# Token sums behind the next item's splits in a macaron transformer kernel, and a conditioning step that starts later

## The chip, the cores and the metric

The kernel runs on one core of one Trainium2 chip. The metric is the device time of one execution in microseconds; the time before is the median of 3 runs.

## The reference, cut to what matters

Two layers work on 768 tokens of width 1024 (256 context tokens, 512 latent tokens). Each layer is a macaron sandwich: half-step SwiGLU FFN, token mixer, half-step SwiGLU FFN. Shift, scale and gate of each sub-layer come from a conditioning vector (adaLN).

```
mx = silu(c) @ ada_w[i] + ada_b[i]                        # 9 rows of 1024 for each layer
def _ffn_sublayer(h, mod, g_pre, g_post, w_in, w_out):
    u = rmsnorm(h, g_pre) * (1 + scale) + shift
    a, b = split(u @ w_in, 2)                             # first gemm: 1024 -> 2 x 2816
    y = (silu(a) * b) @ w_out                             # second gemm: 2816 -> 1024
    return h + 0.5 * gate * rmsnorm(y, g_post)
```

Everything is float32. There are four FFNs: f00 and f01 before and after the attention of layer 0, f10 and f11 those of layer 1. In f11 only the latent tokens are left.

## The kernel before, in words

**Numbers in two parts.** TensorE multiplies in a float32r format; the kernel writes each operand as hi + lo, where hi is a rounded copy made by ScalarE and lo the difference, made by VectorE (`split`, lines 117 to 127; both instructions carry the lines 123 and 126). Each product is three passes, hi·hi, hi·lo and lo·hi (`mm3`). The weights are loaded by `wraw` (three buffers) and split into `whi` and `wlo` (three buffers each, `wpool`, line 78). A buffer comes free when TensorE has read it.

**The first gemm** (`FirstGemm`, line 425) walks over items. The tokens are two sets of three tiles of 128 (two of two tiles in f11). The later items ("R" and "F", `group`, line 553) use a Strassen-like scheme, which multiplies sums of weight blocks with sums of token blocks, so that one item serves both sets of tokens. The token sums T of the second set are made in `to_sums` (line 308) from the normed tokens; they are not ready when the first gemm starts. So it starts with a head: 7, 7, 6 and 5 "E" items (`EARLY`, line 31, for f00, f01, f10 and f11), which need the first set of tokens alone. During the head VectorE and ScalarE make the T sums of the second set's tiles.

An E item is four products. `early_a` (518) multiplies the two weight halves x = 0, 1 with token features 0 to 511, and ScalarE copies the two results out (L529). `early_b` (536) multiplies the halves with features 512 to 1023; VectorE adds the copies (L544), ScalarE takes Silu of the first (L546), VectorE multiplies the two (L548). All four results come out of the two PSUM buffers `psg` (line 80), so a product waits until one of the results before it has been read. Tile names: f01e5x and f01e5v are the PSUM results of item 5 of f01 in early_a and early_b, f015s0h, f015s0l, f015s1h and f015s1l its split weights (half 0 and 1, hi and lo), f01e5s the sums of L544 and L548.

**The steps by which the token sums go on** are a generator in the list `late`; `late_step` (410) runs it to its next yield. Each E item calls it four times: after each product in early_a, after the Silu in early_b, at the end of early_b. For each tile of the second set `to_sums` has three stages: L322 to L328, L331 to L337, L339 to L341; VectorE does L323, L324, L325, then L331, L332, L334, L335, L337, then L339 and L341. With four calls an item, the last tile's second stage falls on the call after Silu of item 4 in f00, f01 and f10, and its third stage on the end of item 4.

**The splits of the next item** are the generator `prep` (459), run by `step`. early_b of item i calls `self.step(i + 1)` first, which splits half 0 of the next item, and `self.step(i + 1, 9)` near its end, which splits half 1.

**The order on an engine** is not the order of the program text. The framework's scheduler builds each engine's queue ahead of time: of the instructions that its own timing holds to be ready it takes the one traced first. An engine then works through its queue strictly in order. `tc.keep_in_program_order(i)` ties instruction i behind whatever was traced before it on the same engine; it adds no wait beyond the queue's order.

**Conditioning.** `mods_pairs` (215) computes the rows of ada_w for later sub-layers during the groups of f00 (3 pairs of rows), f01 (2) and f10 (3). `group` calls `work.step(1)` twice, in its middle (588) and at its end (608). The generator loads two slices of ada_w (`aw`, 1 MB each, two buffers), one on each of its first two steps; then every second step does 8 + 8 matmuls (L245), an add on VectorE (L249), and loads the next two slices. After each pair there is one more step. At the end of an item with x = 1 the stores of the hidden rows (L606, L607) stand on the sync engine's queue (SP) before the step.

Of the kernel before, what the change touches and what calls it, by code (L numbers as in the profile page):

```python
# [9 lines left out]
F32 = mybir.dt.float32  # L10
# [27 lines left out]
PAT1 = "kqVkkqVV"  # L38
PROG0 = "SF1F2b"
PROG1 = "SF12Fb"  # L40
SUMV = (2, 2, 2, 2)
TURN = 1
EVAC = "AA"
JUNK = 1
# [10 lines left out]
def kernel(  # L55
# [19 lines left out]
    nc = tc.nc  # L75
# [32 lines left out]
    def psum_g(name):  # L108
        return psg.tile([P, 512], F32, tag="g", name=name)
# [94 lines left out]
    def pair_loads(pool, pair, k):  # L204
        w = pool.tile([P, 2, D], F32, tag="aw", name=f"aw{pair[0][0]}{pair[0][1]}{k}")
        rows = slice(k * P, (k + 1) * P)
        if pair[0][0] == pair[1][0]:
            l, m = pair[0]
            nc.sync.dma_start(w, ada_w[l, rows, m * D : (m + 2) * D].rearrange("p (a n) -> p a n", a=2))
        else:  # L210
            for a, (l, m) in enumerate(pair):
                nc.sync.dma_start(w[:, a], ada_w[l, rows, m * D : (m + 1) * D])
        return w

    def mods_pairs(pool, pairs):
        seq = [(pair, k) for pair in pairs for k in range(KC)]
        ws, rows = {}, {}

        def load(q):
            if q >= len(seq):  # L220
                return
            pair, k = seq[q]
            nm = f"{pair[0][0]}{pair[0][1]}"
            if k == 0:
                for x, tag in (("b", "mb"), ("g", "araw")):
                    rows[x] = pool.tile([P, 512], F32, tag=tag, name=f"m{x}{nm}")
                    for a, (l, m) in enumerate(pair):
                        row = ada_b[l, m * D : (m + 1) * D] if x == "b" else norm_g[l, g_index[m]]
                        src = bass.AP(tensor=row.tensor, offset=row.offset, ap=[[512, 2], [0, 32], [1, 512]])
                        nc.sync.dma_start(rows[x][64 * a : 64 * a + 64, :], src)  # L230
            ws[q] = pair_loads(pool, pair, k)

        load(0)
        yield
        load(1)
        yield
        for q, (pair, k) in enumerate(seq):
            if k == 0:
                acc, gg = rows["b"], rows["g"]
            if k % 2 == 0:  # L240
                ps = psum_g(f"am{pair[0][0]}{pair[0][1]}{k}")
                for z in range(2):
                    w = ws.pop(q + z)
                    for c in range(4):
                        nc.tensor.matmul(  # L245
                            ps[32 * c : 32 * c + 32], lhsT=s32[:, k + z],
                            rhs=w[:, c // 2, c % 2 * 512 : c % 2 * 512 + 512], start=z == 0, stop=z == 1,
                        )
                nc.vector.tensor_tensor(out=acc, in0=ps, in1=acc, op=ALU.add)  # L249
                load(q + 2)  # L250
                load(q + 3)
            yield
            if k < KC - 1:
                continue
            for a, (l, m) in enumerate(pair):
                r = slice(64 * a, 64 * a + 64)
                if m % 3 == 1:
                    nc.vector.scalar_tensor_tensor(acc[r], acc[r], 1.0, gg[r], ALU.add, ALU.mult)
                elif m % 3 == 2:
                    nc.vector.scalar_tensor_tensor(acc[r], acc[r], 1.0 if m == 5 else 0.5, gg[r], ALU.mult, ALU.mult)  # L260
                for h in range(2):
                    at = 64 * a + 32 * h
                    nc.sync.dma_start(mdram[l][m][:, h * 512 : h * 512 + 512], acc[at : at + 2, :])
                finished.add((l, m))
            yield
# [23 lines left out]
    def by_turn(tp, cols):  # L289
        for k in range(KC):  # L290
            nc.scalar.activation(tp[:, k], tp[:, k], AF.Identity, scale=cols[:, 1, k : k + 1], bias=cols[:, 0, k : k + 1])
# [16 lines left out]
    def to_sums(pool, t, first, un, ps, sums, name, cols=None):  # L308
        tt, sub, add = nc.vector.tensor_tensor, ALU.subtract, ALU.add
        mine = slice(t * P, (t + 1) * P)  # L310
        twin = slice(first * P, (first + 1) * P)
        hi, lo = uhi.bitcast(F32), ulo.bitcast(F32)
        tp = ps.rearrange("p (k n) -> p k n", k=KC) if un is not None else ps
        if un is not None:
            for k in range(KC):
                nc.tensor.transpose(tp[:, k, :], un[:, k * P : (k + 1) * P], ident)
            by_turn(tp, cols)
            yield
        b12, b22 = tp[:, 0:4, :], tp[:, 4:8, :]
        ta = pool.tile([P, 2, 4, P], F32, tag="R1", name=name + "ta")  # L320
        tb = pool.tile([P, 2, 4, P], F32, tag="R1", name=name + "tb")
        nc.scalar.copy(uhi[:, 4:8, mine], b22)  # L322
        tt(out=ta[:, 0], in0=b12, in1=hi[:, 0:4, twin], op=sub)  # L323
        tt(out=ta[:, 0], in0=ta[:, 0], in1=lo[:, 0:4, twin], op=sub)  # L324
        tt(out=ta[:, 1], in0=b22, in1=ta[:, 0], op=sub)  # L325
        th, tl = sums["T"]
        col = slice((t - sums["t2"]) * P, (t - sums["t2"] + 1) * P)
        nc.scalar.copy(th[:, 0:2, :, col], ta)  # L328
        yield
        t4 = tt if sums["vector"] else nc.gpsimd.tensor_tensor  # L330
        t4(out=tb[:, 1], in0=hi[:, 4:8, twin], in1=ta[:, 1], op=sub)  # L331
        t4(out=tb[:, 1], in0=tb[:, 1], in1=lo[:, 4:8, twin], op=add)  # L332
        nc.scalar.copy(tb[:, 0], b12)
        tt(out=tb[:, 0], in0=b22, in1=tb[:, 0], op=sub)  # L334
        tt(out=tl[:, 0:2, :, col], in0=ta, in1=th[:, 0:2, :, col].bitcast(F32), op=sub)  # L335
        nc.scalar.copy(th[:, 2, :, col], tb[:, 0])
        tt(out=ulo[:, 4:8, mine], in0=b22, in1=hi[:, 4:8, mine], op=sub)  # L337
        yield
        tt(out=tl[:, 2, :, col], in0=tb[:, 0], in1=th[:, 2, :, col].bitcast(F32), op=sub)  # L339
        nc.scalar.copy(uhi[:, 0:4, mine], tb[:, 1])  # L340
        tt(out=ulo[:, 0:4, mine], in0=tb[:, 1], in1=hi[:, 0:4, mine], op=sub)  # L341
        yield
# [67 lines left out]
    def late_step(n=1):  # L410
        for _ in range(n):
            while late:
                if next(late[0], "end") == "end":
                    late.pop(0)
                else:
                    break

    def sums_for(pool, sets, name, f):
        n = len(sets[1]) * P
        return {  # L420
            "t1": sets[0][0], "t2": sets[1][0], "vector": SUMV[f] > 1,
            "T": [pool.tile([P, 3, 4, n], F32R, tag=f"T{x}", name=f"{name}T{x}") for x in "hl"],
        }

    class FirstGemm:
# [110 lines left out]
        def early_b(self, i, g):  # L536
            n, pool, nm = self.n, self.pool, f"{self.nm}e{g}"
            a, p1 = self.ops[i], self.p1[i]
            self.step(i + 1)
            sa = [pool.tile([P, 384], F32, tag="h" + "hl"[x], name=f"{nm}s{x}")[:, 0:n] for x in range(2)]  # L540
            for x in range(2):
                ps = psum_g(f"{nm}v{x}")[:, 0:n]
                self.prod(ps, [y[:, 4:8] for y in a[x]], self.cols(self.t1, 4))
                nc.vector.tensor_tensor(out=sa[x], in0=ps, in1=p1[x], op=ALU.add)  # L544
                if x == 0:
                    nc.scalar.activation(sa[0], sa[0], AF.Silu)  # L546
                    late_step()
            nc.vector.tensor_tensor(out=sa[0], in0=sa[0], in1=sa[1], op=ALU.mult)  # L548
            nc.sync.dma_start(hdr[self.slot][2 * g][:, self.t1 * P : self.t1 * P + n], sa[0])
            self.step(i + 1, 9)  # L550
            late_step()
# [782 lines left out]
    def mods(pool, *pairs):  # L1334
        work.add(mods_pairs(pool, [((m // 10, m % 10), (n // 10, n % 10)) for m, n in pairs]))
# [77 lines left out]
    with Main("m0") as mp:  # L1413
# [40 lines left out]
        def second():  # L1454
            hs = [load_h(mp, t, hin_of(t), f"in{t}") for t in full[1]]
            yield
            for t, h in zip(full[1], hs):
                tp = turned(mp, t, h, f"in{t}")
                yield
                us = mp.tile([P, KC, P], F32, tag="AB"[t % 2] + "0", name=f"us{t}")  # L1460
                by_cols("D", us, tp, 0, KC, 0)
                yield
                yield from to_sums(mp, t, t - 3, None, us, more[1], f"in_{t}")
# [87 lines left out]
```

## Time and profile before

| | us |
|---|---|
| median of 3 runs (2819.9 to 2825.96) | 2823.1 |
| the profiled execution's own time | 2828.1 |
| its span, first to last instruction | 2826.1 |
| TensorE matmuls busy in it | 2737.5 (97%) |
| VectorE busy | 1930.6 (68%) |
| ScalarE busy | 1247.4 (44%) |
| GpSimd busy | 754.4 (27%) |

The span is what the trace covers; all moments below are microseconds from its start. PE is TensorE's matmuls, PEld its weight loads, DVE VectorE, ACT ScalarE, POOL GpSimd, SPq the queue of the sync engine, which issues the DMAs. A matmul is shown longer than the time to the next, since they overlap.

### The profile page before, as it was taken

The page shows a single profiled execution, that of the slowest core. Times are in us where ns is not written, and L with a number is a line of the kernel's source. Part 1 is how long each engine was busy: PE and PEld are TensorE (multiplying, and loading weights), DVE is VectorE, ACT ScalarE, POOL GpSimd, SP SyncE. Part 2 cuts the span into 40 slices and gives each one's busy share as a digit, 9 for nine tenths or more (in the row PEclk, how much of TensorE's full clock was granted, in tenths as well). Part 3 has the DMA queues.
Part 4 walks back from the last instruction along what each step waited for, and adds up shares of the span by engine and source line. Part 5 has one row for each costly group of instructions (what it writes and reads, how often), then busy time and mean ns, then how long its engine had stood idle before and what let it go on. Part 6 is the DMA issues. An engine that isn't in the chain of part 4 may idle for free. (4 is left out here: it accounts for less than half of the span.)

```text
span 2826.1 us, 41442 instructions
## 1 busy us (share of the span) xinstructions
PE 2737.5 (97%) x15928; PEld 2436.6 (86%) x15928; DVE 1930.6 (68%) x2550; ACT 1247.4 (44%) x1999; POOL 754.4 (27%) x639
## 2 busy tenths in 40 slices
PE   7999999999998998999999999999999999989999
PEld 6888998888887788899888978998888887789987
DVE  5777755568778587777554867674655556699965
ACT  5322334345556573233344722333444445644444
POOL 0455411000000014554110354430110110177700
PEclk9999999999999999999999999999999999999999
DMA  8786256543333477832665677326644445654375
GB/s 282 254 300 240 100 189 202 189 140 83 92 107 117 154 233 249 292 127 91 221 212 160 211 273 279 136 97 232 219 148 122 120 120 153 216 169 148 123 247 195
DMA packets 318037, 511.60 MB, mean 181 GB/s; under 512 B 28112, under 2 KB 242000, under 8 KB 310672
## 3 DMA queue, kind: packets, MB, share of 16 engines
q1 hardware_dynamic: 317552, 508.31, 54.7%
q8 instruction: 125, 2.05, 0.3%
q14 instruction: 72, 0.59, 0.1%
q10 hardware_dynamic: 288, 0.66, 0.1%
HBM read 410.19 MB, written 63.05 MB: 167 GB/s over the span
## 5 line engine op out<-in xcount | busy, mean ns | idle before, releaser
L1258 POOL TENSOR_TENSOR bias<-bp,nneg 128x128 f32<-128x128 f32 x112 | 50.0, 485 | 285.7 <-DMA nneg<-in_na_neg 94.3
L126 DVE TENSOR_TENSOR f00hl<-f00h,f00hh 128x384 fp32r<-128x384 f32 x44 | 25.6, 582 | 74.2 <-ACT f00hh L123 74.2
L126 DVE TENSOR_TENSOR f01hl<-f01h,f01hh 128x384 fp32r<-128x384 f32 x44 | 25.3, 575 | 74.6 <-ACT f01hh L123 74.6
L126 DVE TENSOR_TENSOR f10hl<-f10h,f10hh 128x384 fp32r<-128x384 f32 x44 | 26.8, 610 | 68.2 <-ACT f10hh L123 68.1
L123 ACT CAST f01hh<-f01h 128x384 fp32r<-128x384 f32 x44 | 22.6, 515 | 112.6 <-PE f01y L732 94.6
L123 ACT CAST f00hh<-f00h 128x384 fp32r<-128x384 f32 x44 | 22.6, 515 | 111.8 <-PE f00y L732 93.0
L245 PE MATMUL am<-aw,s 128*32 128x512 f32 x512 | 64.4, 611 | 7.5 <-DMA aw<-in_ada_w 7.5
L123 ACT CAST f10hh<-f10h 128x384 fp32r<-128x384 f32 x44 | 22.6, 515 | 100.9 <-PE f10y L732 92.5
L131 PE MATMUL av<-pt,davh 128*128 128x256 f32 x224 | 44.0, 290 | 0.6 <-ACT pt L1180 0.6
L245 PEld LDWEIGHTS am<-aw,s 128*32 128x32 f32 x512 | 12.7, 109 | 35.5 <-issue 22.1
L1320 PE MATMUL nav<-npt,navh 128*64 128x256 f32 (+1 forms) x320 | 39.3, 365 | 0.0
L131 PEld LDWEIGHTS av<-pt,davh 128*128 128x128 f32 x224 | 35.8, 191 | 2.4 <-ACT pt L1180 1.0
L123 ACT CAST f11hh<-f11h 128x256 fp32r<-128x256 f32 x44 | 17.8, 405 | 38.4 <-DMA f11h<-hr 25.7
L126 DVE TENSOR_TENSOR f11hl<-f11h,f11hh 128x256 fp32r<-128x256 f32 x44 | 20.3, 464 | 18.0 <-ACT f11hh L123 17.8
L1320 PEld LDWEIGHTS nav<-npt,navh 128*64 128x64 f32 x320 | 22.0, 136 | 12.2 <-issue 1.9
L1105 POOL TENSOR_TENSOR daq0r<-daq0r,rope 128x512 f32<-128x512 f32 x1 | 1.8, 1798 | 114.6 <-DVE daq0s L1104 114.6
L131 PE MATMUL av<-pt,davl 128*128 128x256 f32 x112 | 31.5, 282 | 0.0
L249 DVE TENSOR_TENSOR mb<-am,mb 128x512 f32<-128x512 f32 x32 | 21.8, 682 | 6.4 <-PE am L245 6.2
L285 POOL TENSOR_SCALAR f00y0r<-f00y0s 128x1 f32<-128x1 f32 x1 | 0.2, 192 | 84.5 <-ACT f00y0j L279 84.5
L285 POOL TENSOR_SCALAR f10y0r<-f10y0s 128x1 f32<-128x1 f32 x1 | 0.2, 192 | 84.5 <-ACT f10y0j L279 84.5
L285 POOL TENSOR_SCALAR f01y0r<-f01y0s 128x1 f32<-128x1 f32 x1 | 0.2, 192 | 84.5 <-ACT f01y0j L279 84.5
L285 POOL TENSOR_SCALAR f01y3r<-f01y3s 128x1 f32<-128x1 f32 x1 | 0.2, 192 | 79.3 <-ACT f01y3j L279 79.3
(9729 smaller groups left out, 11477.8 us busy)
## 6 DMA issues: line engine op xcount, KB each, us to landing
aw<-in_ada_w SPq DMA_DIRECT2D x63, 1024.0 KB
f00r<-in_ffn_w_in SPq DMA_DIRECT2D x22, 1024.0 KB
f01r<-in_ffn_w_in SPq DMA_DIRECT2D x22, 1024.0 KB
f10r<-in_ffn_w_in SPq DMA_DIRECT2D x22, 1024.0 KB
f11r<-in_ffn_w_in SPq DMA_DIRECT2D x22, 1024.0 KB
f00o<-in_ffn_w_out SPq DMA_DIRECT2D x21, 1024.0 KB
f01o<-in_ffn_w_out SPq DMA_DIRECT2D x21, 1024.0 KB
f10o<-in_ffn_w_out SPq DMA_DIRECT2D x21, 1024.0 KB
```

The costliest lines, as they stand in the source:

```text
L123: i = nc.scalar.copy(hi, src)
L126: eng.tensor_tensor(out=lo, in0=src, in1=hi.bitcast(F32), op=ALU.subtract)
L131: nc.tensor.matmul(ps, lhsT=lhs[i], rhs=rhs[j], start=first and n == 0, stop=last and n == 2)
L245: nc.tensor.matmul(ps[32 * c : 32 * c + 32], lhsT=s32[:, k + z], rhs=w[:, c // 2, c % 2 * 512 : c % 2 * 512 + 512], start=z == 0, stop=z == 1,
L249: nc.vector.tensor_tensor(out=acc, in0=ps, in1=acc, op=ALU.add)
L285: nc.gpsimd.tensor_scalar(r, ss, 1.0, EPS, ALU.mult, ALU.add)
L1105: nc.gpsimd.tensor_tensor(out=raw, in0=raw, in1=cs[:, 0, :], op=ALU.mult)
L1258: nc.gpsimd.tensor_tensor(out=bias[:, m, :].rearrange("p (a b) -> p a b", a=8), in0=view, in1=neg[:, m, :].rearrange("p (a b) -> p a b", a ...
L1320: nc.tensor.matmul(av[64 * i : 64 * i + 64, half * 256 + c0 : half * 256 + c0 + n], lhsT=made[u]["v"][0][:, key, vc : vc + 64], rhs=made[u ...
```

## The change

It touches five places. (1) In `to_sums` the first VectorE instruction of each of the three stages (L323, L331, L339) is tied behind what was traced before it on VectorE. (2) In `early_b`, where the next item is an E item, the split of its half 1 is traced after the Silu and before the `late_step` there; where the next item is not, it stays at the end. (3) The generator of `mods_pairs` has one more empty step after its second load. (4) The first two instructions of the second stage always go to VectorE. (5) The constant SUMV, whose four entries were all 2 and so chose VectorE for those two everywhere, goes away.

```diff
-SUMV = (2, 2, 2, 2)
...
     def mods_pairs(pool, pairs):
...
         load(1)
         yield
+        yield
         for q, (pair, k) in enumerate(seq):
...
     def to_sums(pool, t, first, un, ps, sums, name, cols=None):
...
-        tt(out=ta[:, 0], in0=b12, in1=hi[:, 0:4, twin], op=sub)
+        tc.keep_in_program_order(tt(out=ta[:, 0], in0=b12, in1=hi[:, 0:4, twin], op=sub))
...
-        t4 = tt if sums["vector"] else nc.gpsimd.tensor_tensor
-        t4(out=tb[:, 1], in0=hi[:, 4:8, twin], in1=ta[:, 1], op=sub)
-        t4(out=tb[:, 1], in0=tb[:, 1], in1=lo[:, 4:8, twin], op=add)
+        tc.keep_in_program_order(tt(out=tb[:, 1], in0=hi[:, 4:8, twin], in1=ta[:, 1], op=sub))
+        tt(out=tb[:, 1], in0=tb[:, 1], in1=lo[:, 4:8, twin], op=add)
...
-        tt(out=tl[:, 2, :, col], in0=tb[:, 0], in1=th[:, 2, :, col].bitcast(F32), op=sub)
+        tc.keep_in_program_order(tt(out=tl[:, 2, :, col], in0=tb[:, 0], in1=th[:, 2, :, col].bitcast(F32), op=sub))
...
     def early_b(self, i, g):
...
                 if x == 0:
                     nc.scalar.activation(sa[0], sa[0], AF.Silu)
+                    if self.items[i + 1][0] == "E":
+                        self.step(i + 1, 9)
                     late_step()
```

## Rows read from the trace of the kernel before

**Rows 1.** The page, part 1: busy time of PE and DVE.

```profile
PE 2737.5 (97%) x15928; PEld 2436.6 (86%) x15928; DVE 1930.6 (68%) x2550; ACT 1247.4 (44%) x1999; POOL 754.4 (27%) x639
```

**Rows 2.** Busy time by stretch: the heads of f00 (from item 2), f01, f10, f11.

```profile
core 0: us, PE busy (x) PEld busy (x) DVE busy (x) ACT busy (x) POOL busy (x), PEclk, DMA share, GB/s
56.20:103.10 46.90, 44.14 (x256) 42.80 (x256) 43.45 (x59) 26.84 (x42) 12.98 (x6) 1.00 0.66 204
1015.60:1089.00 73.40, 65.01 (x362) 63.10 (x361) 56.45 (x70) 50.65 (x89) 14.66 (x17) 0.95 0.68 211
1552.60:1609.10 56.50, 54.37 (x314) 52.40 (x313) 47.73 (x59) 46.33 (x80) 15.96 (x14) 1.00 0.64 202
2446.20:2493.10 46.90, 37.97 (x261) 35.83 (x262) 37.77 (x48) 33.21 (x61) 12.96 (x12) 0.89 0.56 178
```

**Rows 3.** Waits of PE: for whom, us in total, times, longest.

```profile
PE am L245 <- DMA aw<-in_ada_w: 7.5, 6, 2.9
...
PE f01e5x L131 <- DVE f015s1l L126: 5.7, 1, 5.7
...
PE f00a1W L131 <- DVE mb L249: 1.2, 1, 1.2
...
PE f00e5x L131 <- DVE f005s1l L126: 1.1, 1, 1.1
```

**Rows 4.** Timeline of PE in f01: start, us, ...; items 4 to 6.

```profile
1061.94 0.34 PE L131 MATMUL f01e4v<-o0uh,f014s1l 128*128 128x384 f32 x1
1063.33 0.44 PE L131 MATMUL f01e5x<-o0uh,f015s0h 128*128 128x384 f32 x1 [1.05 <-DVE f01e4s L544]
...
1074.34 0.69 PE L131 MATMUL f01e5x<-o0uh,f015s1l 128*128 128x384 f32 x1 [5.71 <-DVE f015s1l L126]
...
1080.65 0.33 PE L131 MATMUL f01e6x<-o0uh,f016s0h 128*128 128x384 f32 x1
1080.82 0.33 PE L131 MATMUL f01e6x<-o0ul,f016s0h 128*128 128x384 f32 x1
```

**Rows 5.** Timeline of ACT in f01: the rounded copy of that half.

```profile
1060.06 1.05 ACT L123 CAST f015s1h<-f01r 128x1024 fp32r<-128x1024 f32 x1 [1.02 <-PE f01e4v L131]
```

**Rows 6.** Timeline of DVE in f01, items 4 and 5.

```profile
1063.80 0.54 DVE L544 TENSOR_TENSOR f01e4s<-f01e4v,f01e4p 128x384 f32<-128x384 f32 x1
1064.26 0.68 DVE L331 TENSOR_TENSOR o_5tb<-o0uh,o_5ta 128x512 f32<-128x512 f32 x1
...
1070.34 1.74 DVE L341 TENSOR_TENSOR o0ul<-o_5tb,o0uh 128x512 fp32r<-128x512 f32 x1
1072.00 2.28 DVE L126 TENSOR_TENSOR f015s1l<-f01r,f015s1h 128x1024 fp32r<-128x1024 f32 x1
...
1075.34 0.54 DVE L544 TENSOR_TENSOR f01e5s<-f01e5v,f01e5p 128x384 f32<-128x384 f32 x1
```

**Rows 7.** Timeline of DVE in f00, items 4 and 5.

```profile
86.25 0.68 DVE L331 TENSOR_TENSOR in_5tb<-inuh,in_5ta 128x512 f32<-128x512 f32 x1
...
89.05 1.22 DVE L126 TENSOR_TENSOR f005s1l<-f00r,f005s1h 128x1024 fp32r<-128x1024 f32 x1
...
92.53 0.55 DVE L544 TENSOR_TENSOR f00e5s<-f00e5v,f00e5p 128x384 f32<-128x384 f32 x1
```

**Rows 8.** First products of f00's items 5 and 6: starts of first and last matmul.

```profile
L131 PE MATMUL f00e5x<-inuh,f005s0h x4: 334/334/334, 83.8 to 85.3; 128*128 128x384 f32 x4
...
L131 PE MATMUL f00e6x<-inuh,f006s0h x4: 334/334/334, 95.1 to 96.7; 128*128 128x384 f32 x4
```

**Rows 9.** Timeline of PE: conditioning matmuls, the first without a wait, in f00, f01 and f10.

```profile
132.63 1.92 PE L245 MATMUL am<-aw,s 128*32 128x512 f32 x16
...
215.57 1.06 PE L245 MATMUL am<-aw,s 128*32 128x512 f32 x8 [1.15 <-DMA aw<-in_ada_w]
...
1200.61 1.07 PE L245 MATMUL am<-aw,s 128*32 128x512 f32 x8 [1.00 <-DMA aw<-in_ada_w]
...
1642.37 1.59 PE L245 MATMUL am<-aw,s 128*32 128x512 f32 x8 [2.93 <-DMA aw<-in_ada_w]
1645.10 1.93 PE L245 MATMUL am<-aw,s 128*32 128x512 f32 x8 [1.13 <-DMA aw<-in_ada_w]
```

**Rows 10.** Timeline of SPq: loads and stores around conditioning steps, in f00 and f10.

```profile
121.29 1.19 SPq L209 DMA_DIRECT2D aw<-in_ada_w  x2
132.37 0.33 SPq L606 DMA_DIRECT2D hr<-f00a0sa  x1
...
1628.87 1.52 SPq L209 DMA_DIRECT2D aw<-in_ada_w  x2
1634.43 0.33 SPq L606 DMA_DIRECT2D hr<-f10a0sa  x1
1638.37 0.33 SPq L607 DMA_DIRECT2D hr<-f10a0sa  x1
```

More of the change, by code (lines that the diff above doesn't have):

```diff
@@ L420, in sums_for @@
         return {
-            "t1": sets[0][0], "t2": sets[1][0], "vector": SUMV[f] > 1,
+            "t1": sets[0][0], "t2": sets[1][0],
             "T": [pool.tile([P, 3, 4, n], F32R, tag=f"T{x}", name=f"{name}T{x}") for x in "hl"],
```

## The prediction

> **What bounds the kernel now.** I read the page first, then busy time by stretch, then PE's waits, then the timelines of DVE, ACT and SPq around the two largest waits that the change can reach. The page says that PE is busy 97% of the span and DVE 68% [rows 1]; on that view nothing that VectorE does could matter. By stretch it looks different [rows 2]: in the four heads PE is busy 44.1 of 46.9, 65.0 of 73.4, 54.4 of 56.5 and 38.0 of 46.9 us, together 22 us idle, while DVE is busy 43.5 of 46.9 us in f00 and 56.5 of 73.4 in f01. The heads are the places where VectorE sets the pace, since it has the splits, the PSUM adds and the token sums to do at once. The list of waits names who is late [rows 3]: the longest single wait of the four rows kept here is 5.7 us for f015s1l, the lo half of the next item's weights, an instruction of VectorE. Its like in f00, f005s1l, costs 1.1 us. Besides, PE waits 7.5 us in 6 places for slices of ada_w, and 1.2 us once in f00 for the add that empties a conditioning result.
>
> **Part 1: the splits ahead of the token sums.** In f01 the hi copy of f015s1 starts at 1060.06 and takes 1.05 us, so f015s1l could have run from 1061.1 [rows 5]. VectorE got to it at 1072.00, after the second and third stage of the last tile's sums, L331 at 1064.26 to L341 at 1070.34 [rows 6]. PE stood until 1074.34 [rows 4]. With the change, L331 is tied behind f015s1l, and the split is traced ahead of the sums of that step; it should then run near 1064, right after the adds of item 4. So this wait goes.
>
> What is late next? One matmul follows another after 0.174 us (1080.65 and 1080.82 are two neighbours) [rows 4], so an item of 4 x 12 takes 8.3 us. Item 5 could start at 1062.1, when item 4's last matmul is through, and item 6 at 1070.4; it started at 1080.65 [rows 4]. So 10.2 us are lost here, and that is the most that can come back. It will not all come back: moving a split ahead of sums takes no work from VectorE. The first product of item 6 needs a PSUM buffer that the add f01e5s empties, and that add started at 1075.34 behind the same sums and splits [rows 6]. VectorE was busy without a break up to there, and in the new order it has the same instructions ahead of that add; it ends at 1075.9 as before. Then item 6 starts at 1075.9 instead of 1080.65: a gain of 4.8 us. The products of item 5, which in the old order came after the late split, now lie beside the sums. I take 4.8, with 10.2 as one end.
>
> f00 has the same shape. f005s1l ran at 89.05, after L331 at 86.25; the add f00e5s started at 92.53 and ended at 93.1 [rows 7]; item 6 started at 95.1 [rows 8]. By the same argument item 6 starts at 93.1: a gain of 2.0 us. Here the most is 3.0 (item 5 starts at 83.8 [rows 8], plus 8.3).
>
> In f10 and f11 the sums of the last tile already run after the next split, or were traced ahead of it before and after the change (f11 has two tiles, and its last stage falls on an earlier product than the moved split). I put them at nothing, between +1 and -1 us each; the 9 us that PE idles in f11 [rows 2] stay.
>
> The other end of part 1: what stands behind a tied instruction waits with it. VectorE works in order, so where f015s1l's hi copy isn't done, the sums and the adds behind them stand still. The nearest row is that copy, 1.05 us [rows 5]; once per head that would cost 4 x 1.05 = 4 us if VectorE had no slack. In f01 the copy was done 3 us before VectorE had finished the adds ahead of it, which is why I take nothing. The sums themselves become later by the split, 1.1 to 2.3 us [rows 6, 7]; whoever needs them, the first group, comes after items 5 and 6, so two items of 8.3 us cover it. If that cover were gone, it would cost those 1.1 to 2.3 us.
>
> Parts (4) and (5) of the change choose what was already chosen, VectorE: nothing.
>
> **Part 2: the conditioning one step later.** No instruction is added. The two first loads are issued as before; the first matmuls of each pair move by half an item, from the middle of an item to its end or back, because each pair has an odd number of steps. So in f00 and f10 pairs 1 and 3, and in f01 pair 1, change from the middle to the end, and pair 2 the other way. What that does:
> - At the end of an item with x = 1 the next two loads stand on SPq behind the stores L606 and L607, while in the middle nothing stands ahead of them. The waits of about 1 us at 215.57 and 1200.61 [rows 9] are of that kind. Taking the pair of waits of f10 (2.93 and 1.13) out of the 7.5 us leaves 3.4 us [rows 3, 9], over the 6 places where a group of a pair 2 followed such loads: 0.58 each. Afterwards there are 10 such places (6 of pairs 1, 4 of pairs 3): 5.8 us, 2.3 more than now.
> - The wait of f00a1W for the add L249 [rows 3], 1.2 us, goes: it arises because in the middle of an item the next two products want the PSUM buffer that the conditioning result holds.
> - The wait of f10 [rows 9], 2.93 + 1.13 us. Its loads left at 1628.87 and the second landed at 1645.1 [rows 9, 10]. Now they leave after L607, at 1638.4, and are wanted two products (24 x 0.174 = 4.2 us) later than the 1639.4 at which PE began to wait, at 1643.6. In f00 two such loads that left at 121.29 were there in time for the group at 132.6, so took 11.3 us or less [rows 9, 10]. With 11.3 the wait is 6.1 us, 2.0 more than now; at the other end there is none, 4.1 less, because the queue had those 10 us to empty. I take 3 us, a gain of 1.0.
>
> Together part 2 comes to +2.3 - 1.2 - 1.0 = +0.1 us, between -5 and +4.
>
> **The sum.** -4.8 - 2.0 + 0.1 = -6.7 us. The profiled execution took 2828.1 us (span 2826.1), 5.0 us above the median of 2823.1; I lay the sum against the median, since nothing in the rows says that the heads were longer in the profiled run than in the others: 2823.1 - 6.7 = 2816.4. About 0.2% (5.6 us) is what a measurement of this kernel can tell from no change, so the forecast lies just beyond that.
>
> The Trainium skill, page "Perfetto Trace Analysis", section "Identifying Performance Opportunities", has a rule against this change: improving a kernel generally means improving its most-contended engine, which by occupancy is the one with the highest share. That is TensorE here, and the change takes nothing from it, so by that rule the time would stay at 2823.1; by the rows of the heads it is 2816.4.
>
> **The rivals.**
> - **The backlog only changes its name (2821).** VectorE's work in the heads stays the same, so PE could wait as long for the adds as it did for the splits. For it: DVE is busy 43.5 of 46.9 us in f00 [rows 2], and item 5 of f01 already waited 1.05 us for such an add [rows 4]. Against it: the 6 us from 1068 to 1074, in which PE had nothing at all, would be filled by item 5's remaining products. Then f01 gives 2 us (what is left of 4.8 if the add comes as much later as the split, 2.3 us, and a little more) and f00 none: 2821. This is also what becomes of the time if the scheduler places the sums elsewhere in the queue, so that the change does not do what it says. Chance 0.24.
> - **More comes back (2811).** The adds get ahead of the third stage, which is now tied behind the product L548; f01 gives 8 us of its 10.2, f00 2, and the wait of f10 goes altogether (4.1, against +1.1 from the other two points of part 2): -8 - 2 - 3 = -13, about 2810.5. For it: DVE is busy for only 56.5 of the 73.4 us of f01's head [rows 2], so there is slack elsewhere in it. Chance 0.20.
> - **The loads are caught behind the stores (2835).** The place is the end of the first x = 1 group in f00, f01 and f10. In f00 its first store left only at 132.37 [rows 10]; loads behind it would leave at 133.2 and, with 11.3 us, land at 144.5, while the group that wants them stands at 136.8 (132.6 + 4.2) [rows 9]: 7.7 us, the same in f01, and 2.0 in f10. Sum: -6.8 + 2.3 - 1.2 + 17.4 = +11.7, about 2835. It decides when the stores leave: after 125.5 in f00 (136.8 - 11.3) PE waits, before it nothing happens. Against it: the stores were late because VectorE's add stood behind a prefetch that shared the DMA queues with those very loads (issued at 121.29, ahead of the stores), and with the loads gone from there it should be early. Chance 0.14.
>
> **How the numbers follow.** The forecast has 0.42, the rivals 0.24, 0.20 and 0.14. The range reaches from 2808 (the larger gain, with 2.5 us for f10 and f11) to 2827 (nothing in the heads, +4 from part 2), and leaves out most of the third rival. Faster by over 0.2%: two thirds of the forecast and the second rival, 0.28 + 0.20 = 0.48. Within 0.2%: the rest of the forecast and the first rival, 0.14 + 0.24 = 0.38. Slower: 0.14.
>
> **What would show it.** In the profile after: f015s1l and f005s1l ahead of L331 of the last tile on DVE; no wait of PE for them; item 6 of f01 starting some 12.6 us after item 5 instead of 17.3, that of f00 some 9.3 after instead of 11.3; the mean clock of f01's head above 0.95. The conditioning matmuls of the first pair stand behind the last product of an item, without the wait of f00a1W. Wrong would be: PE waits for f01e5s as long as it did for f015s1l (first rival); a wait of over 5 us for ada_w in the second group of f00 or f01 (third rival); a head of f10 or f11 that is longer by more than 1 us, since I found nothing there that the change moves.

## The result and the profile after

The changed kernel took 2837.95 us (median of four runs, 2836.84 to 2843.45), the kernel before 2823.78 us beside it (four runs, 2819.9 to 2825.96): a ratio of 1.0052, 95% interval 1.0039 to 1.0065. I had forecast 2816.4, in a range of 2808 to 2827. It is slower by 14 us, outside the range and on the other side of no change.

The profiled execution took 2836.84 us (span 2834.7), 8.6 us of span more than that of before, the shortest of the four runs shown, against one of before that was longer than its four. So the two traces differ by 8.6 us and not by 14. The page hardly moves: PE's sum is 1.8 us less than in [rows 1], DVE's 7.0 more. Line numbers after are one less than before up to the extra `yield`, the same from there to L325, one less again from L331 to L546, and one more from L548 on; the runs below have their own.

```profile
PE 2735.7 (97%) x15928; PEld 2433.9 (86%) x15928; DVE 1937.6 (68%) x2550; ACT 1245.5 (44%) x1999; POOL 754.7 (27%) x639
```

I laid the two traces beside each other by the start of the first matmul of each product. The shift (after minus before) grows and falls like this: up to f00's head +0.5; over f00's head +3.9; over its groups +3.9; to f01's start +1.0; over f01's head -4.2; over its groups +3.5; over f10's head and first item +4.1; over f10's other groups +0.7; in f10's second gemm and the attention behind it -3.0; in f11 -1.8. Together 8.6. Most of the -3.0 seems to lie in the one execution of before that was profiled: the traces of all the runs below are 1.0 to 3.6 us shorter than it there, too. Of the heads, only f01's does what I forecast.

Busy time by stretch, from the same points as [rows 2] (columns as there): f00's head is 51.1 us long instead of 46.9, f01's 69.2 instead of 73.4.

```profile
56.70:107.80 51.10, 46.18 (x257) 44.52 (x257) 45.60 (x59) 27.16 (x42) 9.74 (x6) 0.97 0.65 198
1024.90:1094.10 69.20, 63.24 (x362) 60.66 (x362) 56.19 (x70) 50.57 (x89) 15.87 (x17) 1.00 0.74 228
```

PE's waits after, answering to [rows 3]. The waits for f015s1l, f005s1l and f00a1W are gone; in their place stand waits for adds (f00e5s, f10e4s, b0c; before, f10e4s cost 0.5), and that for ada_w has grown from 7.5 to 10.5 us.

```profile
PE am L245 <- DMA aw<-in_ada_w: 10.5, 10, 4.7
...
PE f00e6x L130 <- DVE f00e5s L543: 3.2, 1, 3.2
...
PE f10e5x L130 <- DVE f10e4s L543: 2.8, 1, 2.8
...
PE am L245 <- DVE f01b0c L560: 2.4, 1, 2.4
...
PE am L245 <- DVE f00b0c L560: 2.2, 1, 2.2
...
PE f01e6x L130 <- DVE f01e5s L543: 1.4, 1, 1.4
```

**f01's head.** DVE's timeline after, the answer to [rows 6]: f015s1l stands ahead of the sums L330, and the add f01e5s at 1085.00 lets item 6 start at 1085.60, 12.6 us after item 5 (at 1072.99). That is what I had written.

```profile
1073.45 1.21 DVE L125 TENSOR_TENSOR f015s1l<-f01r,f015s1h 128x1024 fp32r<-128x1024 f32 x1
1074.58 0.68 DVE L330 TENSOR_TENSOR o_5tb<-o0uh,o_5ta 128x512 f32<-128x512 f32 x1
...
1079.53 1.77 DVE L340 TENSOR_TENSOR o0ul<-o_5tb,o0uh 128x512 fp32r<-128x512 f32 x1
1081.22 0.54 DVE L543 TENSOR_TENSOR f01e4s<-f01e4v,f01e4p 128x384 f32<-128x384 f32 x1
1081.69 1.83 DVE L125 TENSOR_TENSOR f016s0l<-f01r,f016s0h 128x1024 fp32r<-128x1024 f32 x1
...
1085.00 0.55 DVE L543 TENSOR_TENSOR f01e5s<-f01e5v,f01e5p 128x384 f32<-128x384 f32 x1
```

**f00's head.** The same order, another outcome. The split is early here too (84.91), but the four instructions between the adds f00e4s and f00e5s take 1.30, 1.64, 1.77 and 2.28 us. Their likes take 0.68 (L341), 0.55 (L548), 0.68 (L339) and 1.22 (f006s0l) in f00's trace of before: 3.9 us more. DVE before, DVE after, POOL before and POOL after:

```profile
86.84 0.55 DVE L548 TENSOR_TENSOR f00e4s<-f00e4s,f00e4s 128x384 f32<-128x384 f32 x1
...
90.19 0.68 DVE L339 TENSOR_TENSOR inTl<-in_5tb,inTh 128x512 fp32r<-128x512 f32 x1
90.79 0.68 DVE L341 TENSOR_TENSOR inul<-in_5tb,inuh 128x512 fp32r<-128x512 f32 x1
91.39 1.22 DVE L126 TENSOR_TENSOR f006s0l<-f00r,f006s0h 128x1024 fp32r<-128x1024 f32 x1
```

```profile
84.91 1.22 DVE L125 TENSOR_TENSOR f005s1l<-f00r,f005s1h 128x1024 fp32r<-128x1024 f32 x1
...
90.19 0.55 DVE L543 TENSOR_TENSOR f00e4s<-f00e4v,f00e4p 128x384 f32<-128x384 f32 x1
90.66 1.30 DVE L340 TENSOR_TENSOR inul<-in_5tb,inuh 128x512 fp32r<-128x512 f32 x1
91.89 1.64 DVE L549 TENSOR_TENSOR f00e4s<-f00e4s,f00e4s 128x384 f32<-128x384 f32 x1
93.45 1.77 DVE L338 TENSOR_TENSOR inTl<-in_5tb,inTh 128x512 fp32r<-128x512 f32 x1
95.14 2.28 DVE L125 TENSOR_TENSOR f006s0l<-f00r,f006s0h 128x1024 fp32r<-128x1024 f32 x1
97.35 0.54 DVE L543 TENSOR_TENSOR f00e5s<-f00e5v,f00e5p 128x384 f32<-128x384 f32 x1
```

```profile
88.35 5.40 POOL L479 TENSOR_TENSOR f007s<-f00r 128x512 f32<-128x512 f32 x1 [32.83 <-DMA f00r<-in_ffn_w_in]
```

```profile
89.28 2.12 POOL L478 TENSOR_TENSOR f007s<-f00r 128x512 f32<-128x512 f32 x1 [33.26 <-DMA f00r<-in_ffn_w_in]
...
94.75 1.59 POOL L481 TENSOR_TENSOR f007s<-f00r,f007s 128x512 f32<-128x512 f32 x1
```

After, GpSimd makes the sums of the first group's weights (f007s) at that very time. PE waits 3.2 us for the add, and after the wait the granted clock is 0.71 and 0.86 for two stretches of 4 us (it was 1.00 in both before): a matmul follows the last after 0.32 us (98.43, 98.75), at the lower of the clock's two levels (1.2 GHz), instead of 0.174 at the upper (2.4 GHz), so item 6 takes 9.9 us instead of 8.3. PE's timeline after, then windows of it, PE alone:

```profile
97.95 0.69 PE L130 MATMUL f00e6x<-inuh,f006s0h 128*128 128x384 f32 x1 [3.20 <-DVE f00e5s L543]
98.43 0.52 PE L130 MATMUL f00e6x<-inul,f006s0h 128*128 128x384 f32 x1
98.75 0.52 PE L130 MATMUL f00e6x<-inuh,f006s0l 128*128 128x384 f32 x1
```

```profile
96.00:100.00 4.00, 2.05 (x6) 0.71 0.93 219
100.00:104.00 4.00, 4.00 (x21) 0.86 0.51 162
```

**The first groups.** In the first x = 1 item, DVE has f00hl to do: the split of the second gemm's first hidden rows (the second gemm's `prep`), moved ahead into these groups by the scheduler. The load of those rows leaves at 115.75 and ACT's copy f00hh can start only at 126.71. DVE after:

```profile
121.09 0.55 DVE L560 TENSOR_TENSOR f00b0u<-f00b0X,f008p 128x384 f32<-128x384 f32 x1
127.26 0.56 DVE L125 TENSOR_TENSOR f00hl<-f00h,f00hh 128x384 fp32r<-128x384 f32 x1 [5.62 <-ACT f00hh L122]
127.73 0.55 DVE L560 TENSOR_TENSOR f00b0c<-f00b0u,f00b0Z 128x384 f32<-128x384 f32 x1
```

Before, the same instruction stood five places later, behind three adds of that item and behind the add L249 that empties the conditioning result, and PE had no wait for any of them while DVE stood still for 4.99 us:

```profile
122.94 0.68 DVE L249 TENSOR_TENSOR mb<-am,mb 128x512 f32<-128x512 f32 x1
128.60 0.56 DVE L126 TENSOR_TENSOR f00hl<-f00h,f00hh 128x384 fp32r<-128x384 f32 x1 [4.99 <-ACT f00hh L123]
129.08 0.55 DVE L559 TENSOR_TENSOR f00b0c<-f00b0c,f00b0Z 128x384 f32<-128x384 f32 x1
```

After these waits the granted clock falls as well: behind the 2.2 us of f00 it is 0.59 from 132 to 136, behind the 2.4 us of f01 0.79 from 1116 to 1124, where it was 1.00 before. By these shares that is some 1.6 us each (an estimate: 4 x 0.41 and 8 x 0.21); with the waits, which sum to 2.0 us more than before in either place, it comes close to the 3.9 and 3.5.

In f10 the stores, too, wait for DVE: it stands still for 6.0 us (1642.9 to 1648.9, for ACT's f108dh, which stands behind f10hh), L607 and L608 leave at 1652, the loads of ada_w behind them, and PE waits 4.74 us (1656.3 to 1661.05). SPq after:

```profile
1652.19 0.32 SPq L607 DMA_DIRECT2D hr<-f10a0sa  x1
1652.61 0.38 SPq L608 DMA_DIRECT2D hr<-f10a0sa  x1
1653.11 1.12 SPq L208 DMA_DIRECT2D aw<-in_ada_w  x2
```

### The profile page after: what moved, and what is told of

Same layout as the page of the kernel before. It is cut to its first block, busy times and chain, and to the rows that moved or that the text cites. A ratio compares the mean times of both kernels' runs of the same rounds, so it can differ in the third digit from the quotient of the medians.

```text
span 2834.7 us, 41432 instructions
## 1 busy us (share of the span) xinstructions
PE 2735.7 (97%) x15928; PEld 2433.9 (86%) x15928; DVE 1937.6 (68%) x2550; ACT 1245.5 (44%) x1999; POOL 754.7 (27%) x639
## 5 line engine op out<-in xcount | busy, mean ns | idle before, releaser
L245 PE MATMUL am<-aw,s 128*32 128x512 f32 x512 | 67.4, 626 | 15.1 <-DMA aw<-in_ada_w 10.5
L122 ACT CAST f00hh<-f00h 128x384 fp32r<-128x384 f32 x44 | 22.6, 515 | 103.7 <-PE f00y L733 93.1
L245 PEld LDWEIGHTS am<-aw,s 128*32 128x32 f32 x512 | 12.7, 110 | 46.9 <-issue 20.1
L249 DVE TENSOR_TENSOR mb<-am,mb 128x512 f32<-128x512 f32 x32 | 21.8, 681 | 6.6 <-PE am L245 6.6
L130 PEld LDWEIGHTS av<-pt,davl 128*128 128x128 f32 x112 | 21.7, 193 | 0.0
```

Of the source, the lines that this page charges most:

```text
L122: i = nc.scalar.copy(hi, src)
L130: nc.tensor.matmul(ps, lhsT=lhs[i], rhs=rhs[j], start=first and n == 0, stop=last and n == 2)
L245: nc.tensor.matmul(ps[32 * c : 32 * c + 32], lhsT=s32[:, k + z], rhs=w[:, c // 2, c % 2 * 512 : c % 2 * 512 + 512], start=z == 0, stop=z == 1,
```

## The experiments

**Head and step apart.** "Heads" below is the change without its extra empty step, "step" the kernel before with that step alone, "rows held" the edit of the third run.

```diff
         load(1)
         yield
-        yield
```

> The change to the heads alone: the extra empty step of the conditioning generator is taken out again, so that its first matmuls stand where they stood before. Theory (the later step costs the time): the first conditioning groups cost PE 3.9, 3.5 and 7.7 us more from the first group's first item to the second gemm's first in f00, f01 and f10; without the step these 15 us go, and what is left is the heads: f00 about 4 us longer, f01 about 4.8 shorter, f10 and f11 within 3 either way, so about 2820 to 2825, at most 0.1% from before. PE's waits for b0c's add (2.2 and 2.4 us) are gone and the longest wait for ada_w is again about 2.9 us. Rival (the order in the heads costs the time): it stays at 2833 to 2838.

Measured: 2835.03 us, ratio 1.0037 (1.0024 to 1.0050). The theory fell: without the step the 15 us don't go. Its trace shows why. The heads cost what they did (f00's +5.1, f01's -4.2, f10's with its first item +3.2), and the split of the hidden rows still stands ahead of b0c's adds, since the scheduler places it the same way. Now the conditioning result is what isn't emptied: the add L248 stands behind it, and PE waits 2.9 us in f00 and 2.7 in f01 for it, at b0W. DVE of this run:

```profile
121.91 0.55 DVE L559 TENSOR_TENSOR f00b0u<-f00b0X,f008p 128x384 f32<-128x384 f32 x1
128.67 0.56 DVE L125 TENSOR_TENSOR f00hl<-f00h,f00hh 128x384 fp32r<-128x384 f32 x1 [6.22 <-ACT f00hh L122]
...
131.80 0.68 DVE L248 TENSOR_TENSOR mb<-am,mb 128x512 f32<-128x512 f32 x1
```

```diff
         load(1)
         yield
+        yield
```

> The kernel before with the extra empty step alone, the heads as they were. Theory (the later step costs the time): slower by 11 to 15 us, 2834 to 2839; PE waits some 2 us in f00 and in f01 for b0c's add, which stands on DVE behind the split of the second gemm's first hidden rows, and over 4 us in f10 for ada_w. Rival (the order in the heads costs the time): within 3 us of before, 2821 to 2827, and none of these waits. If both this and the other run come out in the middle, the two parts share the loss.

Measured: 2841.14 us, ratio 1.0058 (1.0045 to 1.0070): slower by 17 us, 2 more than the theory's upper end, and no less than both parts together. So their prices can't be added. The waits are not those I had written. In f00 DVE stands still for 5.36 us for ACT's copy f009dh, which stands behind f00hh; the next conditioning group waits 3.3 us for a split of DVE (f0011bl) and 1.1 for ada_w, and behind that the granted clock is 0.60 and 0.55 for two stretches of 4 us. In f01, where the stores leave only at 1123.95, the loads behind them (1124.84) come 2.5 us late: the third rival's place.

**The rows held.** `prep` of the second gemm's first rows gets `stay=True`, so that ACT's hi copies keep their place in the program.

```diff
-            split(hraw[q][:, 0:n], None, "", [y[:, 0:n] for y in hh])
+            split(hraw[q][:, 0:n], None, "", [y[:, 0:n] for y in hh], stay=stay)
...
         for _ in plan[0][1]:
-            prep(q)
+            prep(q, True)
```

> The changed kernel, with the hi copies of the second gemm's first hidden rows kept where the program has them, so that they and the splits behind them can't be moved ahead into the first groups. Theory (b0c's add and the stores stand behind that split, which stands behind a load): DVE's idle stretches of 5.6 and 5.8 us ahead of b0c's add in f00 and f01 go, and with them PE's 2.2 and 2.4 us; in f10 the stores L607 and L608 leave some 6 us earlier, and the 4.7 us wait for ada_w falls below 1.5: together 6 to 9 us, less up to 3 us at the start of each second gemm, whose first split is now late: 2829 to 2834. Rival (the matmuls are late because of their own loads or buffers, whatever DVE waits for): no change, 2836 to 2840, and the same waits under other names.

Measured: 2823.79 us, ratio 0.9998 (0.9989 to 1.0008): as much as the whole loss goes, more than expected. DVE is no longer blocked ahead of b0c, the adds come when PE has their products, and no wait for b0c is left. The longest wait for ada_w falls from 4.7 to 1.3 us. From the last group of f00 to the start of f01 the shift grows by 1.5 us (1.0 in the changed kernel), so the late split costs little. But not all that goes is the change's loss. f11's groups are 3.6 us shorter than before, and the change had moved nothing there (0.0): before and after it, f11's hidden rows, too, are split among these groups, ahead of the weights' split f119cl (before, f11hl starts at 2521.89 and takes 2.61 us), and PE waits for that and for f1110cl and f1112cl. All nine runs with the rows held gain 3.2 to 3.9 us there. DVE of this run:

```profile
123.80 1.22 DVE L125 TENSOR_TENSOR f009cl<-f009s,f009ch 128x1024 fp32r<-128x1024 f32 x1
124.94 0.55 DVE L560 TENSOR_TENSOR f00b0c<-f00b0c,f00b0Z 128x384 f32<-128x384 f32 x1
125.40 1.53 DVE L125 TENSOR_TENSOR f009dl<-f00r,f009dh 128x512 fp32r<-128x512 f32 x1
```

The cells that are missing beside these are three more runs: the same edit on the kernel before, on the heads and on the step.

> The kernel before, with the hi copies of the second gemm's first hidden rows kept where the program has them; heads and conditioning as before. Theory (the split of those rows, moved ahead into the first groups, blocks DVE for 4 to 6 us while its load is on the way; before, PE paid for it only by the 1.2 and 0.5 us waits for the conditioning result and by part of the 4.1 us for ada_w in f10): faster by 3 to 5 us, 2819 to 2821. Rival (the split has a cost of its own at the second gemm's start, or PE's waits are the loads' own): within 2 us of before, 2822 to 2826.

Measured: 2820.4 us, 0.9982 (0.9973 to 0.9991): the size that the theory gave, but mostly in another place. PE's waits for the conditioning result are gone, but in the trace the groups of f00 gain 1.1 us and those of f01 0.5, those of f10 lose 1.2, and its longest wait for ada_w is still 3.1; f11's groups gain 3.5, where PE's waits for f1110cl and f1112cl fall from 1.7 to 0.9 us each and that for f119cl (1.6) goes. So the size was in part luck.

> The change to all heads, the conditioning at its old step, and the second gemm's first rows held. Theory (the loss of the heads alone, 11 us, is 5 us in f00's head, 4 in f10's, minus 4.5 in f01's, and 3.8 to 4.3 in each of the first groups of f00 and f01, where the split of those rows had come to stand ahead of b0c's adds): the 8 us of the first groups go, and 3 to 5 us of the heads stay: 2822 to 2828. Rival (the loss of the heads alone is in the heads): it stays at 2833 to 2837. Against the run with the rows held and the later step (2823.8) it shows the step alone: within 3 us if its cost was only the place of that split, 6 or more apart if the step has a price of its own.

Measured: 2820.25 us, 0.9981 (0.9970 to 0.9992), better than the 2822 to 2828 expected; the 8 us of the first groups are gone, and the 3.6 of f11's groups, which I had not counted. Against the run with the later step (0.9998) the step alone is 0.0017, 5 us.

> The kernel before with the rows held and the extra empty step, heads as before: the cell still missing among heads, step and rows. Theory (most of the step's loss of 16 us is the split that stands ahead of what empties its buffers; what is left is its own price, 3 to 4 us, which the two runs with changed heads and held rows differ by): 2822 to 2825. Rival (the step has a price of its own that the changed heads hide): 2828 or more.

Measured: 2822.68 us, 0.9991 (0.9982 to 0.9999), as the theory said.

Ratio to the kernel before:

| | as it was | rows held |
|---|---|---|
| neither | 1 | 0.9982 |
| heads | 1.0037 | 0.9981 |
| step | 1.0058 | 0.9991 |
| both (the change) | 1.0052 | 0.9998 |

In the left column each part costs 0.4 to 0.6% and the two together no more. In the right column, against its own first row, the heads cost nothing, the step 0.1 to 0.2%, both 0.16%. So some 10 of the 15 us are the place of the split of the hidden rows and of the ScalarE copy in front of it: both parts of the change brought PE to stand behind them, by different buffers. The other 5 are the step's (2.5 alone, 5 beside the changed heads), and the whole of the loss goes only because holding the rows gains about as much by itself.

**f00 as before.** Heads as in the first run, but in f00 neither ties nor the earlier split.

```diff
-        tc.keep_in_program_order(tt(out=ta[:, 0], in0=b12, in1=hi[:, 0:4, twin], op=sub))
+        keep = tc.keep_in_program_order if sums["keep"] else (lambda i: i)
+        keep(tt(out=ta[:, 0], in0=b12, in1=hi[:, 0:4, twin], op=sub))
...
-                    if self.items[i + 1][0] == "E":
+                    if self.items[i + 1][0] == "E" and self.nm != "f00":
```

> The change to the heads alone, and in f01, f10 and f11 only: f00 keeps the order of before (no ties, no earlier split), and the conditioning has its old step. Theory (in f00 the displaced sums of the last tile run beside GpSimd's sums of the first R/F item and are slowed by them, 1.2 to 1.8 us an instruction): f00's head is again 4 us shorter than in the run with the order changed in all heads, so 4 us faster than that run, 2816 to 2821. Rival (f00's head grew for another reason, the clock or the loads): the same time as that run within 1 us.

Measured: 2831.95 us, 1.0025 (1.0014 to 1.0035): 3.1 us less than with all heads, of the 4 expected. f00 is as before up to its last group (+0.8 us), while the first run's trace had lost 8.3 there. The forecast of 2816 to 2821 failed: by the trace f01's head gains 3.7 us and its first groups give 3.6 of them back behind the same split, and f10's head and first item lose 3.2.

**GpSimd's sums left out.** On heads with the rows held, the first group's four sums in f00 are replaced by raw slices.

```diff
+            if self.nm == "f00" and i == 7:
+                s12 = r[:, :, 0:P].rearrange("p (x k) n -> p x k n", x=2)
+                s34 = r[:, :, P:256].rearrange("p (x k) n -> p x k n", x=2)
+            else:
```

> As the run with all heads changed, the old step and the rows held, but GpSimd's four sums of the first group's weights after the heads' items in f00 are left out (the raw slices stand in their place, so that group of f00 computes something else). Theory (GpSimd's sums stretch the VectorE instructions that run beside them): L339, L548, L337 and f006s0l fall from 1.31, 1.64, 1.77 and 2.28 us to about 0.68, 0.55, 0.68 and 1.22, so that the add f00e5s starts some 3.9 us earlier, PE's wait of 3.2 us before f00e6x goes, f00e6x starts 3 us earlier against f00e5x, and the time falls by 3 to 5 us. Rival (VectorE is late there by the order alone): the wait stays above 2 us and the time within 1.5 us.

Measured: 2817.41 us, 0.9975 (0.9965 to 0.9986). Its base has 0.9981, so the times alone don't tell the two apart, and the 3 to 5 us expected did not come; the traces tell them apart. The four instructions fall to 0.68, 0.55, 0.69 and 1.22 us, PE's 3.2 us are gone, the clock of the two stretches is 1.00, and f00's head ends 1.1 us earlier than before instead of 4.5 later. Item 6 now starts without a wait, at 94.03, as soon as item 5 is through. DVE of this run:

```profile
90.09 0.68 DVE L339 TENSOR_TENSOR inul<-in_5tb,inuh 128x512 fp32r<-128x512 f32 x1
90.69 0.55 DVE L552 TENSOR_TENSOR f00e4s<-f00e4s,f00e4s 128x384 f32<-128x384 f32 x1
91.16 0.69 DVE L337 TENSOR_TENSOR inTl<-in_5tb,inTh 128x512 fp32r<-128x512 f32 x1
91.77 1.22 DVE L125 TENSOR_TENSOR f006s0l<-f00r,f006s0h 128x1024 fp32r<-128x1024 f32 x1
92.90 0.55 DVE L546 TENSOR_TENSOR f00e5s<-f00e5v,f00e5p 128x384 f32<-128x384 f32 x1
```

The same in f10:

```diff
-            if self.nm == "f00" and i == 7:
+            if self.nm == "f10" and i == 6:
```

> As the run with all heads changed, the old step and the rows held, but GpSimd's four sums of the first group's weights after the heads' items are left out in f10 (that group of f10 then computes something else). Theory (in f10, too, VectorE is stretched by them, and that is why f10e5x waits 2.8 us for the add f10e4s): the stretched instructions (1.7 to 1.8 us) fall to 0.68 and 1.22, the wait falls below 1 us, and the time is 2 to 4 us less than that run's. Rival (the add is late by the order alone): the wait stays above 2 us and the time within 1.5 us.

Measured: 2821.92 us, 0.9988 (0.9980 to 0.9997), and the wait is 2.8 us as it was. My theory for f10 isn't shown. The instructions that had been stretched are short again, but the next group's sums moved up into the gap (1596.63 to 1604.85) and stretch others (f105s0l 1.72, L323 1.75). So the run doesn't separate the two; a kernel with no sums of GpSimd there at all was not tried. The other traces speak for the order: before, too, GpSimd stretched four VectorE instructions of this head, by 3.2 us together (L332, L335, L339 and L341 took 1.20, 2.31, 1.16 and 1.78), after it was 3.1 (L330, L549, L331 and L334), and the wait was 0.5 and 2.8. What differs is that two sums of the last tile (L323, L324), 1.2 us, now stand ahead of the add f10e4s; before they stood behind it. The rest stays open.

```profile
PE f10e5x L130 <- DVE f10e4s L546: 2.8, 1, 2.8
```

**f01 alone.** The order changed in f01 alone, the old step, the rows held.

```diff
-            "t1": sets[0][0], "t2": sets[1][0],
+            "t1": sets[0][0], "t2": sets[1][0], "keep": f == 1,
...
-                    if self.items[i + 1][0] == "E":
+                    if self.items[i + 1][0] == "E" and self.nm == "f01":
```

> The order of the heads changed in f01 alone, the conditioning at its old step, and the second gemm's first rows held. Theory (f01's head gains its 4.2 to 4.8 us, and gives nothing back once no split can stand ahead of b0c's adds; the rows give 3 to 5): faster by 7 to 10 us, 2814 to 2817. Rival (what f01's head gains is given back in its first groups for another reason): like the kernel before with rows held alone, 2819 to 2822.

Measured: 2815.41 us, 0.9963 (0.9950 to 0.9976), faster than both kernels. Its two halves, first the ties alone:

```diff
-                    if self.items[i + 1][0] == "E" and self.nm == "f01":
-                        self.step(i + 1, 9)
```

> As the run with the order changed in f01 alone and the rows held, but only the three ties are changed there; the next item's split is traced where it was. Theory (what brings f01's 5 us back is that the sums of the last tile stand behind f015s1l on DVE, and the ties do that by themselves): f015s1l again runs ahead of L331, no wait of 5 us for it, and the time stays within 2 us of that run, 2813 to 2818. Rival (the earlier place in the trace does it): f015s1l is late as in the kernel before, PE waits some 5 us for it, and the time is that of before with the rows held, 2818 to 2822.

Measured: 2820.48 us, 0.9982 (0.9973 to 0.9990). The rival is right: the ties alone leave f015s1l where it was, at 1071.69 behind L340, and PE waits for it:

```profile
PE f01e5x L130 <- DVE f015s1l L125: 4.2, 1, 4.2
```

Then the split alone:

```diff
-            "t1": sets[0][0], "t2": sets[1][0], "keep": f == 1,
+            "t1": sets[0][0], "t2": sets[1][0], "keep": False,
```

> The other half: in f01 the next item's split is traced earlier, without the ties; rows held, conditioning as before. Theory (the ties bring the gain): f015s1l stays behind the sums, PE waits 5 us for it, 2818 to 2822. Rival (the place in the trace brings it): no such wait, 2813 to 2818.

Measured: 2815.85 us, 0.9969 (0.9957 to 0.9981). The earlier place in the trace does all of it; the ties add nothing that can be measured. In the trace f01's head is 4.9 us shorter from item 5 to its end. DVE of this run:

```profile
1062.96 1.21 DVE L125 TENSOR_TENSOR f015s1l<-f01r,f015s1h 128x1024 fp32r<-128x1024 f32 x1
1064.09 0.68 DVE L330 TENSOR_TENSOR o_5tb<-o0uh,o_5ta 128x512 f32<-128x512 f32 x1
```

## Why the prediction was wrong

Two parts of the sum failed: f00's head, -2.0, was +3.9, since VectorE's instructions took longer in the new order; and the first groups, where the sum has +0.1 for the step, lost some 10 us to a wait that no term holds: PE waits for PSUM buffers whose adds stand on VectorE behind the split of the hidden rows, which waits for a load.

- **f01's head, -4.8:** right, in size (-4.2 in the trace) and by its own steps: split early, item 6 bound by the add f01e5s. Its clock is 1.00, over the 0.95 that I named (before, it was 0.59 and 0.55 from 1072 to 1080, behind the 5.7 us wait). "L331 is tied behind f015s1l" was wrong as a cause: the split's earlier place brings the gain.
- **f00's head, -2.0: +3.9.** The failed step is "by the same argument item 6 starts at 93.1". I took DVE's work ahead of the add to be the same in the new order, with the durations of the old one. The instructions were the same, their durations were not: beside GpSimd's sums they took 3.9 us more, and the clock after PE's 3.2 us wait took 1.6 us on top. With those sums left out f00's head does gain, 1.1 us. The 2.0 could not come even then: it has item 6 start 9.3 us after item 5, and item 5 alone takes 10.1 (84.45 to 94.58 after, 83.89 to 94.03 without the sums), in part since PE waits twice 0.57 us in it for ScalarE's copies. That GpSimd started there at 88.35 before, and that its first sum took 5.40 us, stood in the trace; the prediction makes nothing of it.
- **f10, "nothing, between +1 and -1": +4.1** over the head and first item in the profiled execution, the sign of being wrong that I had named. I looked at the last tile's second stage alone; its first two sums (L323, L324) now stand ahead of the add f10e4s. PE's wait for that add grew from 0.5 to 2.8 us, in part for a reason that stays open, and behind it the clock is 0.50 and 0.67 from 1610 to 1618 (1.00 before). f11 (-1.8) is a little outside the range that I gave it; nothing was tried there.
- **The step, +0.1 between -5 and +4.** The terms of the sum were the wrong ones. f00a1W's 1.2 us did go; the waits at the ends of x = 1 items came as something else. I asked who loads late and never asked what the conditioning matmuls' own PSUM buffer waits for at its new place: it waits for b0c's add, behind a split that waits for a load. With the rows held, the step costs 2.5 to 5 us instead of 17.
- **"With the loads gone from there it should be early".** This is how I argued the third rival down to 0.14, and it failed. The stores stayed late (f10: 1652.19), since DVE stands still for f00hh and its likes. Their load was no faster with the ada_w loads gone from there: in f00 it took 11.0 us (115.75 to 126.71), and 7.6 before (120.41 to 128.06). That rival named the right block (a prefetch ahead of VectorE's add) and the right sign; its waits of 7.7 us for ada_w in f00 and f01 didn't come; there PE was held up earlier, by the add itself (2.2 and 2.4 us). In f10 the wait came: 5.3 us (4.74 and 0.56) in place of the 4.1 of before [rows 9]. That the rival's 2835 lies near the 2837.95 is luck.
- **The sum.** I added the heads and the step as if they were apart. They meet in one place, the split of the hidden rows: alone they cost 11 and 17 us, together 14; with the rows held, by the ratios and against the kernel before with the rows held, nothing, 2.5 and 4.5. The heads move that split, though the diff doesn't touch it: tying and retracing a few DVE instructions let the scheduler put it five places further ahead. (A slip beside it: the second rival's -8 - 2 - 3 gives 2810.1, not 2810.5.)
- **The rule cited against the change.** The section of the Trainium skill that the prediction cites there, "Identifying Performance Opportunities" of "Perfetto Trace Analysis", speaks less against the change than I made it: it goes on to the gaps of the engine and what it waits for in them, which is what the change was after. The 2823.1 that I drew from it was missed as well: PE's busy sum is 1.8 us less and the time 14 us more.

## What to carry to other kernels

An in-order engine that stands still "at no cost" is a debt: DVE's 5 us ahead of f00hh were hidden before, and two small shifts elsewhere called them in. Before costing a moved step, list what each of its instructions waits for at the new place, buffers included, and what stands ahead of the instruction that frees them; look at the idle time of that engine, even where nobody waits for it yet. And when work is moved on VectorE, look at what GpSimd does at the new time, since durations from the old order don't carry over.

## What the runs showed of the hardware

VectorE and GpSimd slow each other, and which of the two pays differs between the two orders. In f00 before, GpSimd's first sum took 5.40 us (88.35 to 93.75) while VectorE's instructions beside it kept 1.22 and 0.68 us; after, VectorE's took up to 2.28 and 1.77 us and GpSimd's 1.6 to 2.1. The Trainium skill, page "SBUF — State Buffer", section "Who interferes with whom", says that the two share a pair of ports, that a VectorE instruction with two inputs in SBUF contends with a GpSimd instruction that reads SBUF, one with at most one such input (outside the modes that use both ports) does not, and that issue order decides who blocks. The traces agree: between the two stretched instructions of f01 (1.77 and 1.83 us, while GpSimd runs), the add L543, whose one input is PSUM, keeps its 0.54 us. It also fits that GpSimd's 5.40 us end (93.75) just after the first such add of VectorE in that stretch (92.53 to 93.08): no instruction of one SBUF input stood between them before, while after one stands at 90.19. That the add let GpSimd in is argued from these times; no run tested it alone.

A wait of PE of 2 to 3 us can cost more than itself. Five of the profiled runs have the 3.2 us wait in f00. In four of them the granted clock is lower behind it (0.71 and 0.86 in the two 4 us stretches from 96 to 104, the same in the heads with the rows held, 0.56 and 0.58 in the heads alone, 0.61 and 0.54 in the run without GpSimd's sums in f10), and item 6 takes 9.8 to 11.2 us. In the fifth, the change with the rows held, it stays at 1.00 and item 6 takes 8.45 us. So the same wait comes with and without that price.
